# An eighth depth pair by seven products in the late heads, and a third raw weight buffer in the room of the descriptor reserve

## The chip, the cores and the metric

The kernel runs on one core of a Trainium2 chip. The metric is the device time in microseconds of one execution, as the median of several runs. TensorE (PE in the profile, its weight loads PEld), VectorE (DVE), ScalarE (ACT), GpSimd (POOL) and the queue of SyncE (SP), which issues all transfers, each work through their own list of instructions in a fixed order.

## The reference

Two layers over 512 tokens of width 2048, each a sandwich-normalised mixer with an adaptive shift, scale and gate from a conditioning vector. The first is an mLSTM with eight heads, the second an attention over a band of chunks with sixteen heads, which reads keys and values computed from the residual stream after the first layer. All matrices are float32. The part that the change touches is the first layer's input projection:

```python
proj = h @ w_in
qk = jax.nn.silu(causal_conv(proj[..., :A_V0], conv_w, conv_b))
v = proj[..., A_V0:A_O0]
o = proj[..., A_O0:A_Z0]
z = proj[..., A_Z0:A_G0]
...
y = jax.nn.sigmoid(o) * ht * jax.nn.silu(z)      # ht: the normalised mLSTM output
return y @ w_out
```

`h` is 512 x 2048. Per head there are 256 columns of q, 256 of k, and 512 each of v, o and z.

## The kernel before, in words

**Three matmuls for one.** A float32 product is made of float32r parts: `split` (L202) casts a tile to `hi` on ScalarE and takes the rest as `lo` on VectorE; `mm3` (L276) adds hi x hi, hi x lo and lo x hi.

**The weight stream.** All weights lie in one array in the order in which they are used (`stream`, L73). A piece is 128 x 1024 (some smaller). `raw_load` (L214) issues its transfer from SP into a buffer with the tag `raw`; `wpiece` (L224) makes `hi` and `lo` of it (three buffers each). There are `RAW_BUFS` = 2 raw buffers in the pool `wp`. Where a pool of the current stage is entered as `spare[0]`, every third piece goes to one more raw buffer in that pool: so in the start, the heads up to the q/k columns of head 3, the first output projection, the key stage and the second output projection from its second column group on. From the values of head 3 to the end of head 7, in the attention and in the first group of the second output projection `spare[0]` is `None`, and there are two.

**Seven products for eight.** For a pair of output column blocks (128 columns each) and a pair of depth blocks (k, k+1), with the tokens in two halves, the four block products times two token halves can be had from seven half-length products, as in Winograd's form of Strassen's method. `proj_s` (L319) does it: with `f` of the eight depth pairs by seven products of 256 columns, and the others (`eight`, L338) by four plain products of 512 columns. Each of these products is three matmuls. The four accumulators D, C, A, B are put together after the last piece (L368 on ScalarE, L369 to L377 on VectorE). `pair_pieces` (L50) orders the pieces: with f = 7 the first piece holds one depth pair for seven products and the plain one, the other three hold two pairs for seven products. For each piece the sums of weight blocks are taken on VectorE (L244, L245, L246) into a tile `ws`, whose split (`wsh`, `wsl`) follows that of the piece itself. The sums of input blocks (`h1s`) are made once, by `head_sums` (L708), one depth pair at a call; it also overwrites the second token half of `h1[2k]` with the sum of both blocks.

**V after the sums.** Since that half is overwritten, V (`proj_b`, L295) uses for the tokens of the second half the difference of two weight blocks in place of the second block, for the depth pairs that are already summed (`summed`): L251 makes the difference on VectorE, and its split follows.

**The heads.** Heads 0 to 2 have plain projections. Head 3 (`HALF`) has plain q, k and v; its four o/z column pairs are a ramp with f = 4, 5, 6, 7 (`RAMP`), and a call of `head_sums` at the second piece of a pair raises the number for the next one. Heads 4 to 7, the late heads, have `f = HEAD_PAIRS` = 7 in the two q/k pairs and in the four o/z pairs. A head's order on TensorE is q/k, V with the scores, o/z, the denominators and the mixing `ps_n`, then the next head's q/k with the sum of squares (`ps_q`) put in between. After it VectorE takes a reciprocal (L872) and scales the head's output (L874), and SP stores it (L875). Later stages are the output projection, values, keys (f = 6, 7, then 8), attention (f = 8 for all 16 heads) and the second output projection.

**Who sets the order.** A planner in the compiler orders each engine's instructions once, from a cost model, priorities and the free buffers; `tc.high_priority(AHEAD)` moves weight work and the accumulators' reading forward, `pin` and `keep_in_program_order` fix an order. On the chip the lists are followed as they stand.

**Memory.** The program's constructor is called without a size for the dynamic DMA scratch, which reserves 16 KB of each partition for descriptors.

Of the kernel before, what the change touches and what calls it, by code (L numbers as in the profile page):

```python
# [9 lines left out]
F32 = mybir.dt.float32  # L10
# [5 lines left out]
P = 128  # L16
# [14 lines left out]
REL = 257  # L31
EXTW = 640
AHEAD = 300
RAW_BUFS = 2

PAIRS = [(0, 1), (2, 3)]
BLOCKS = [(0, 2), (2, 6), (6, 12), (12, 16)]
# [3 lines left out]


KEY_PAIRS = [6, 7, 8, 8, 8, 8, 8, 8]
HEAD_PAIRS = 7
RAMP = [4, 5, 6, 7]
HALF = 3
ATT_PAIRS = 8
# [25 lines left out]
def stream():  # L73
# [25 lines left out]
    for h in range(NH):  # L99
        for c in (h * DK, V0 // 2 + h * DK):  # L100
# [3 lines left out]
            elif h > HALF:  # L104
                tile_s("a_w_in", c, c + P, HEAD_PAIRS, True)
        tile_b("a_w_in", V0 + h * DV)
        if h >= HALF:
            for i in range(4):
                tile_s("a_w_in", O0 + h * DV + i * P, Z0 + h * DV + i * P, HEAD_PAIRS if h > HALF else RAMP[i], True)
        elif h:  # L110
# [36 lines left out]
def hybrid_trunk(ctx, tc, xT, xN, c, adaT, cols, wst, wg, ext, kc, out):  # L147
    nc = tc.nc
# [8 lines left out]
    def pool(name, bufs=1, **kw):  # L157
        return tc.tile_pool(name=name, bufs=bufs, reuse_waits="tile", **kw)

    wp = ctx.enter_context(tc.tile_pool(name="wp", bufs=3, side="right"))  # L160
# [46 lines left out]

    parted, first, stock = [None, None], [], []
    ahead = [0]
    spare = [None]  # L210
    loads = []
    pin = tc.keep_in_program_order

    def raw_load(keep=lambda ins: ins):  # L214

        i, at = wpos
        n = sum(w for _, _, w in order[i][1])
        wpos[:] = i + 1, at + P * n
        own = spare[0] and i % (RAW_BUFS + 1) == 0
        raw = (spare[0] if own else wp).tile([P, 1024], F32, tag="raw", name=f"wr{i}", bufs=1 if own else RAW_BUFS)[:, :n]  # L220
        keep(nc.sync.dma_start(raw, wst[at : at + P * n].rearrange("(p n) -> p n", p=P)))
        loads.append(raw)

    def wpiece(mat, groups=(), pl=None, bufs=(2, 2), diff=False, early=False):  # L224

        if stock and not early:
            return stock.pop(0)()
        i = wpos[0] - len(loads)  # L230
        m, blocks = order[i]
        assert m == mat
        n = sum(w for _, _, w in blocks)
        with tc.high_priority(ahead[0]):
            if not loads:
                raw_load()
            raw = loads.pop(0)
            ts = []
            c0 = 0
            for j, ns in enumerate(groups):  # L240
                w = ns * P
                r = raw[:, c0 : c0 + 4 * w]
                t = pl.tile([P, 3 * w], F32, tag="ws", name=f"ws{i}_{j}", bufs=bufs[0])
                nc.vector.tensor_tensor(t[:, : 2 * w], r[:, w : 3 * w], r[:, : 2 * w], op=ALU.subtract)  # L244
                nc.vector.tensor_tensor(r[:, w : 2 * w], t[:, w : 2 * w], r[:, :w], op=ALU.add)  # L245
                nc.vector.tensor_tensor(t[:, 2 * w :], r[:, 3 * w :], r[:, w : 2 * w], op=ALU.subtract)  # L246
                ts.append(t)
                c0 += 4 * w
            if diff:
                t = pl.tile([P, n // 2], F32, tag="ws", name=f"ws{i}", bufs=1)  # L250
                nc.vector.tensor_tensor(t, raw[:, n // 2 :], raw[:, : n // 2], op=ALU.subtract)  # L251
                ts.append(t)
            hi = wp.tile([P, 1024], F32R, tag="hi", name=f"wh{i}")[:, :n]
            lo = wp.tile([P, 1024], F32R, tag="lo", name=f"wl{i}")[:, :n]
            if i == 0:
                pin(nc.scalar.copy(hi, raw))

                def rest():
                    parted[0] = nc.vector.tensor_tensor(lo, raw, hi.bitcast(F32), op=ALU.subtract)
                    behind(parted[0], first[0])  # L260
                    return [(hi, lo)]

                return rest
            parted[:] = split(hi, lo, raw, *first[1:] if i < 3 else ())
            out = [(hi, lo)]
            for j, t in enumerate(ts):
                sh = pl.tile(list(t.shape), F32R, tag="wsh", name=f"wsh{i}_{j}", bufs=bufs[1])
                sl = pl.tile(list(t.shape), F32R, tag="wsl", name=f"wsl{i}_{j}", bufs=bufs[1])
                split(sh, sl, t)
                out.append((sh, sl))  # L270
        return out
# [151 lines left out]
    mst = ExitStack()  # L423
# [4 lines left out]
    hst = ExitStack()  # L428
    acp = hst.enter_context(pool("acc"))
    st = ExitStack()  # L430
    sp = spare[0] = st.enter_context(pool("start"))
    def ada_load(i, p, n, pin=lambda ins: ins, parts=1, js=None):

        w = D // parts
# [34 lines left out]
    for q in range(4):  # L469
        t = sp.tile([P, 4, S], F32, name=f"xt{q}")  # L470
# [68 lines left out]
    h1 = []  # L539
# [25 lines left out]
    for n, step in enumerate(steps):  # L565
# [22 lines left out]
        k0, k1, i0, g = step  # L588
# [11 lines left out]
    st.close()  # L600
    ahead[0] = AHEAD

    bp = spare[0] = mst.enter_context(pool("ada1", side="right"))
    hp = hst.enter_context(pool("head"))
    aT = hp.tile([P, 4, NH], F32, name="aT")
    ones_r = hp.tile([P, P], F32R, name="ones_r")
# [99 lines left out]
    h1s = []  # L706

    def head_sums():  # L708
# [3 lines left out]
        for t in h1[2 * k : 2 * k + 2]:  # L712
            r = tp.tile([P, S], F32, tag="t", name=f"h1r{k}_{len(raw)}")
            nc.vector.tensor_tensor(r, t[:, 0, :].bitcast(F32), t[:, 1, :].bitcast(F32), op=ALU.add)
            raw.append(r)
        h1s.append(three_sums(raw, hq, f"h1s{k}", HEAD_PAIRS, h1[2 * k][:, :, 256:]))

    def pair(c, name, other, f=HEAD_PAIRS, at={}):
        z1, z2 = (acp.tile([P, 2, 256], F32, tag="so", name=f"{name}_{i}", bufs=6) for i in range(2))
        proj_s("a_w_in", h1, h1s, f, z1, z2, name, hq, (1, 2), at, True, other)  # L720
        return [z.rearrange("p a t -> p (a t)") for z in (z1, z2)]

    def scores(h, j, qk, pr, nm, nmd, tot):
# [30 lines left out]
    for h in range(NH):  # L754
# [18 lines left out]
        if h == HALF:  # L773
            while loaded or pending:
                background(2)
            spare[0] = None
            mst.close()
            hqst = ExitStack()
            hq = hqst.enter_context(pool("hq", side="right"))
# [13 lines left out]
        at = {8 + 2 * j: lambda j=j: scores(h, j, qk, pr, nm, nmd, tot) for j in range(4)} if h else {}  # L793
# [13 lines left out]
        for m in range(4):  # L807
            with tc.high_priority(AHEAD):
                if m < 3:
                    t = hp.tile([P, 2, S], F32R, tag="qk", name=f"v{h}_{m}", bufs=4)  # L810
                    split(t[:, 0, :], t[:, 1, :], pv[m])
                else:
                    t = hp.tile([P, S], F32, tag="nm", name=f"v{h}_{m}")
# [6 lines left out]
        for i in range(4):  # L820
            if h >= HALF:
                f = HEAD_PAIRS if h > HALF else RAMP[i]
# [65 lines left out]
    tst = ExitStack()  # L888
    tp = tst.enter_context(pool("t2", bufs=6, side="right"))
    rst = ExitStack()  # L890
    rp = spare[0] = rst.enter_context(pool("rp", bufs=12, side="right"))

    ys = []

    def y_tile(k):
        while len(ys) <= k:
            h, q = divmod(len(ys) // 2, 2)
            with tc.high_priority(AHEAD):
                if len(ys) < 4:
                    raw = wp.tile([P, 2, S], F32, tag="raw", name=f"yr{h}_{q}", bufs=RAW_BUFS)  # L900
                    nc.sync.dma_start(raw, ysc[h, :, 2 * q : 2 * q + 2, :])
# [127 lines left out]
    for pair, ms in enumerate(PAIRS):  # L1029
        for g in range(1, 4):  # L1030
            at = scale_steps(4, 12, 20, *([28] if g < 3 else [])) if pair == 0 else {}
            if pair == 0 and g == 3:
                at[28] = lambda: (scale_sums(), amul_cols(2, 48 + KT, GPRE + KT))
            if pair == 1 and g == 1:
                at = {2: lambda: residual(0), 4: lambda: residual(1)}
                at |= {20 + 4 * i: lambda i=i: turned(0, [i], False) for i in range(3)}
            if pair == 1 and g == 2:
                at = {2: lambda: turned(0, [3], False)}
            if pair == 1 and g == 3:
                at = {k: lambda k=k: [key_input(i, kept(i, slice(0, 2 * P)), slice(0, 2 * P)) for i in range(k // 2 - 1, k // 2 + 1)] for k in range(2, 32, 4)}  # L1040
# [48 lines left out]
    for pair, ms in enumerate(PAIRS):  # L1089
        for g in range(2):  # L1090
# [1 line left out]
            if pair:  # L1092
                turn = {k: input_sums for k in (2, 6, 12)}
            values(g, ms, turn)
    spare[0] = None
    rst.close()
    zst = ExitStack()
    zp = zst.enter_context(pool("zp", bufs=2, side="right"))
    zxst = ExitStack()
    zx = zxst.enter_context(pool("zx", side="right"))  # L1100
    for i in range(KT // 2):
        z = zp.tile([P, 4, 256], F32, tag="z", name=f"zk{i}")
        ready = len(hs)
        at = {2: input_sums} if ready < KT // 2 else {}
        assert ready == KEY_PAIRS[i]
        spare[0] = zp
        proj_s("kv_w", hkv, hs, ready, z[:, 0:2, :], z[:, 2:4, :], f"k{i}", zx, (2, 2), at, True, i % 2 == 1)
        nc.sync.dma_start(ksc[i].rearrange("p a t -> p (a t)"), z.rearrange("p a t -> p (a t)"))
    zxst.close()
# [3 lines left out]
    for g in range(2, 4):  # L1113
        n = -(-ATT_PAIRS // 2)
# [3 lines left out]
    for k in range(0, KT, 2):  # L1118
        raw = []
# [9 lines left out]
            h2s[k // 2][0] = h2[k][:, :, 256:]  # L1129
        for i in range(2):  # L1130
            split(h2[k + i][:, 0, :], h2[k + i][:, 1, :], raw[i])
    spare[0] = None
    zst.close()
    tst.close()

# [1 line left out]
    at = ast.enter_context(pool("att"))  # L1137
# [122 lines left out]
    rp = ost.enter_context(pool("x2", bufs=8))  # L1260
# [11 lines left out]
    def y2_tile(k):  # L1272
        while len(y2) <= k:
            i = len(y2) // 2
            raw = wp.tile([P, 2, S], F32, tag="raw", name=f"y2r{i}", bufs=RAW_BUFS) if i < 2 else op.tile([P, 2, S], F32, tag="yr", name=f"y2r{i}", bufs=2)
            with tc.high_priority(AHEAD):
# [45 lines left out]
        3: {0: lambda: gate_part(0), 2: lambda: (gate_row(1, 3), fetch_x(3)), 6: lambda: gate_row(1, 0, late[1]), 12: gate_first},  # L1322
    }
    for g in range(4):
        if g:
            spare[0] = rp
        for pair in [range(4)] if g < 3 else PAIRS:
            ps = [newp(f"ps_y1_{g}_{m}") for m in pair]
            at = {4: lambda: finish(0), 6: lambda: finish(1)} if pair == PAIRS[1] else {}
            add_at(at, gate_steps[g] if pair != PAIRS[1] else {})  # L1330
            proj_b("b_w_out", y2_tile, ps, ms=pair, at=at, late=3 if pair == PAIRS[1] else 0)
            with tc.high_priority(AHEAD):
                for p, m in zip(ps, pair):
                    yo[m].append(op.tile([P, S], F32, tag="o", name=f"yo{m}_{g}"))
                    evac(p, m, g, yo[m][g], g > 0, last if g == 3 and pair == PAIRS[1] else None)
# [59 lines left out]
```

## Time and profile before

| | |
|---|---|
| median of 3 runs | 2782.41 us |
| lowest and highest | 2779.46 and 2782.7 us |
| the profiled execution, span from the first to the last instruction | 2780.8 us |
| TensorE busy | 2757.6 us (99%), 16186 matmuls |
| VectorE busy | 2180.5 us (78%) |
| ScalarE busy | 1388.8 us (50%) |
| HBM | 190 GB/s over the span |

What the profiled execution took around its span is not shown on the page. Busy time of TensorE is modelled from pipelined matmuls, so the time that one matmul costs in a stream is read from the number of matmuls in a stretch without holes, not from the mean duration of one. In rows of busy time by stage the columns are: the stretch in microseconds from the span's start, its length, then for TensorE, weight loads, VectorE, ScalarE and GpSimd the busy time and (x) the number of instructions, the granted clock of TensorE, the DMA engines' busy share and GB/s. In rows of the order of work they are: start, duration, engine, line, operation, output and inputs, shapes, and in brackets the engine's idle time before it and what ended it.

### The profile page before, as it was taken

The numbers are of one execution on the slowest core, as the hardware profiler recorded it, in microseconds if no ns is written. First come the engines' busy times: TensorE is split into PE (matmuls) and PEld (weight loads), VectorE is DVE, ScalarE is ACT, GpSimd is POOL, SyncE is SP. The second block draws the span as 40 slices with busy tenths as digits, with TensorE's granted clock in tenths as the row PEclk, the third lists the DMA queues.
The fourth block names the chain that finished last, engine by engine and source line by source line (L and its number), as shares of the span: only waits on it lengthen the run. The fifth ranks groups of instructions, "written<-read, shape, count | busy, mean of one in ns | idle before, by whom it ended". The sixth has DMA issues, their size and how long they took to land.

```text
span 2780.8 us, 41974 instructions
## 1 busy us (share of the span) xinstructions
PE 2757.6 (99%) x16186; PEld 2446.3 (88%) x16186; DVE 2180.5 (78%) x3421; ACT 1388.8 (50%) x1993; POOL 0.2 (0%) x4
## 2 busy tenths in 40 slices
PE   8999999999999999999999999999999999999998
PEld 6887888888998989989999888888998899999877
DVE  8975978669897887878878676567976788898666
ACT  4243624234554554555645334568534466666523
POOL 0000000000000000000000000000000000000000
PEclk9999999999999999999999999999999999999999
DMA  9754687855233232232326799788535534334686
GB/s 367 292 202 136 246 303 265 300 205 195 92 116 106 100 123 98 101 116 102 120 93 215 236 293 301 250 269 286 175 130 187 162 129 129 125 124 129 214 308 243
DMA packets 167874, 527.05 MB, mean 190 GB/s; under 512 B 17989, under 2 KB 33893, under 8 KB 155001
## 3 DMA queue, kind: packets, MB, share of 16 engines
q1 hardware_dynamic: 167674, 524.38, 54.6%
q8 instruction: 126, 2.06, 0.3%
q14 instruction: 74, 0.61, 0.1%
HBM read 490.69 MB, written 38.85 MB: 190 GB/s over the span
## 4 chain that ended last, share of the span: by engine, by line
PE 91%; DVE 5%; DMA 3%; issue 1%; ACT 1%; SPq 0%; DVEq 0%; ACTq 0%
PE ps_y L274 17%; PE ps_v L274 12%; PE ps_kv L274 5%; PE ps_azo L274 5%; PE ps_o L274 4%; PE ps_czo L274 3%; PE ps_dzo L274 3%; PE ps_az L274 3%; PE ps_cz L274 3%; PE ps_dz L274 3%; PE ps_qk L274 3%; PE ps_z L274 3%; PE ps_l L274 3%; PE ps_bzo L274 3%; PE ps_s L274 2%; PE ps_n L274 2%
## 5 line engine op out<-in xcount | busy, mean ns | idle before, releaser
L203 ACT CAST wh<-wr 128x1024 fp32r<-128x1024 f32 (+1 forms) x560 | 580.0, 1037 | 734.9 <-PE ps_y L274 217.0
L203 DVE TENSOR_TENSOR wl<-wr,wh 128x1024 fp32r<-128x1024 f32 (+1 forms) x560 | 674.5, 1206 | 337.2 <-ACT wh L203 335.6
L274 PE MATMUL ps_y<-wh,y 128*128 128x512 f32 x1536 | 476.7, 390 | 0.5 <-ACT sqy L927 0.5
L274 PEld LDWEIGHTS ps_y<-wh,y 128*128 128x128 f32 x1536 | 288.2, 188 | 60.8 <-ACT sqy L927 1.0
L203 ACT CAST wsh<-ws 128x768 fp32r<-128x768 f32 (+2 forms) x236 | 178.8, 757 | 260.4 <-PE ps_az L274 124.0
L274 PE MATMUL ps_y<-wl,y 128*128 128x512 f32 x768 | 299.0, 389 | 0.0
L274 PE MATMUL ps_v<-wh,h 128*128 128x512 f32 x912 | 289.6, 390 | 0.0
L203 DVE TENSOR_TENSOR wsl<-ws,wsh 128x768 fp32r<-128x768 f32 (+2 forms) x236 | 203.0, 860 | 72.8 <-ACT wsh L203 71.3
L445 DVE CUSTOM_DVE_ANT_0 ada<-ada,scB,cl 128x2048 f32<-128x2048 f32 (+1 forms) x96 | 222.6, 2325 | 18.3 <-DMA ada<-in_adaT 18.3
L274 PEld LDWEIGHTS ps_v<-wh,h 128*128 128x128 f32 x912 | 171.2, 188 | 34.9
L274 PE MATMUL ps_v<-wl,h 128*128 128x512 f32 x456 | 177.9, 390 | 0.0
L274 PEld LDWEIGHTS ps_y<-wl,y 128*128 128x128 f32 x768 | 144.3, 188 | 29.3
L274 PE MATMUL ps_kv<-wh,hkv 128*128 128x512 f32 x512 | 159.3, 390 | 0.0
L244 DVE TENSOR_TENSOR ws<-wr 128x256 f32<-128x256 f32 (+1 forms) x208 | 133.1, 640 | 7.2 <-DMA wr<-in_wst 5.3
L274 PEld LDWEIGHTS ps_kv<-wh,hkv 128*128 128x128 f32 x512 | 96.1, 188 | 19.7
L274 PEld LDWEIGHTS ps_v<-wl,h 128*128 128x128 f32 x456 | 85.7, 188 | 17.8 <-issue 0.9
L274 PE MATMUL ps_kv<-wl,hkv 128*128 128x512 f32 x256 | 99.7, 390 | 0.0
L274 PE MATMUL ps_l<-h,wh 128*128 128x512 f32 x320 | 98.5, 390 | 0.0
L246 DVE TENSOR_TENSOR ws<-wr 128x128 f32<-128x128 f32 (+1 forms) x208 | 83.0, 399 | 4.0
L245 DVE TENSOR_TENSOR wr<-ws,wr 128x128 f32<-128x128 f32 (+1 forms) x208 | 82.6, 397 | 2.9
L274 PE MATMUL ps_azo<-h,wh 128*128 128x256 f32 (+1 forms) x372 | 84.1, 314 | 0.0
L274 PE MATMUL ps_qk<-h,wh 128*128 128x512 f32 x256 | 79.3, 390 | 0.0
(408 smaller groups left out, 6354.1 us busy)
## 6 DMA issues: line engine op xcount, KB each, us to landing
wr<-in_wst SPq DMA_DIRECT2D x530, 512.0 KB, 3.5
ada<-in_adaT SPq DMA_DIRECT2D x94, 1024.0 KB, 6.3
ada<-in_adaT SPq DMA_DIRECT2D x36, 512.0 KB, 7.6
adq<-in_adaT SPq DMA_DIRECT2D x64, 256.0 KB, 4.7
xt<-nsc SPq DMA_DIRECT2D x48, 256.0 KB, 4.3
wr<-in_wst SPq DMA_DIRECT2D x26, 384.0 KB, 3.1
yr<-ysc SPq DMA_DIRECT2D x28, 256.0 KB, 7.1
bsc<-in_ext SPq DMA_DIRECT2D x16, 320.0 KB, 5.1
```

The costliest lines, as they stand in the source:

```text
L203: ins = nc.scalar.copy(hi, src), nc.vector.tensor_tensor(lo, src, hi.bitcast(F32), op=ALU.subtract)
L244: nc.vector.tensor_tensor(t[:, : 2 * w], r[:, w : 3 * w], r[:, : 2 * w], op=ALU.subtract)
L245: nc.vector.tensor_tensor(r[:, w : 2 * w], t[:, w : 2 * w], r[:, :w], op=ALU.add)
L246: nc.vector.tensor_tensor(t[:, 2 * w :], r[:, 3 * w :], r[:, w : 2 * w], op=ALU.subtract)
L274: return nc.tensor.matmul(ps, a, b, start=start, stop=stop)
L445: pin(nc.vector.tensor_tensor_reduce(c, c, (sc or scB)[:, j * w : (j + 1) * w], 1.0, mod[:, i : i + 1] if j else col(CB + i), ALU.mult, AL ...
```

## The change

The reserve for descriptors goes from 16 KB to 1 KB of each partition. `HEAD_PAIRS` goes from 7 to 8: all depth pairs of the late heads' q/k and o/z columns go by seven products, V of these heads takes eight differences instead of seven, and the ramp of head 3 calls `head_sums` once more, in its last pair. The raw buffers are three everywhere, all in `wp`, and the lent buffer (`spare`) goes. The sums' tile `ws` has two buffers in the late heads instead of one.

```diff
-RAW_BUFS = 2
+RAW_BUFS = 3
...
-HEAD_PAIRS = 7
+HEAD_PAIRS = 8
...
-        own = spare[0] and i % (RAW_BUFS + 1) == 0
-        raw = (spare[0] if own else wp).tile([P, 1024], F32, tag="raw", name=f"wr{i}", bufs=1 if own else RAW_BUFS)[:, :n]
+        raw = wp.tile([P, 1024], F32, tag="raw", name=f"wr{i}", bufs=RAW_BUFS)[:, :n]
...
-                t = pl.tile([P, n // 2], F32, tag="ws", name=f"ws{i}", bufs=1)
+                t = pl.tile([P, n // 2], F32, tag="ws", name=f"ws{i}", bufs=2)
...
-        proj_s("a_w_in", h1, h1s, f, z1, z2, name, hq, (1, 2), at, True, other)
+        proj_s("a_w_in", h1, h1s, f, z1, z2, name, hq, (2, 2), at, True, other)
...
-    nc = bacc.Bacc("TRN2", target_bir_lowering=False, num_devices=1)
+    nc = bacc.Bacc("TRN2", target_bir_lowering=False, num_devices=1, dynamic_dma_scratch_size=1024)
```

The other lines of the diff take out the assignments to `spare[0]`.

More of the change, by code (lines that the diff above doesn't have):

```diff
@@ L209, in hybrid_trunk @@
     ahead = [0]
-    spare = [None]
     loads = []
@@ L430, in hybrid_trunk @@
     st = ExitStack()
-    sp = spare[0] = st.enter_context(pool("start"))
+    sp = st.enter_context(pool("start"))
     def ada_load(i, p, n, pin=lambda ins: ins, parts=1, js=None):
@@ L601, in hybrid_trunk @@
     ahead[0] = AHEAD
-    bp = spare[0] = mst.enter_context(pool("ada1", side="right"))
+    bp = mst.enter_context(pool("ada1", side="right"))
     hp = hst.enter_context(pool("head"))
@@ L775, in hybrid_trunk @@
                 background(2)
-            spare[0] = None
             mst.close()
@@ L890, in hybrid_trunk @@
     rst = ExitStack()
-    rp = spare[0] = rst.enter_context(pool("rp", bufs=12, side="right"))
+    rp = rst.enter_context(pool("rp", bufs=12, side="right"))
     ys = []
@@ L1094, in hybrid_trunk @@
             values(g, ms, turn)
-    spare[0] = None
     rst.close()
@@ L1105, in hybrid_trunk @@
         assert ready == KEY_PAIRS[i]
-        spare[0] = zp
         proj_s("kv_w", hkv, hs, ready, z[:, 0:2, :], z[:, 2:4, :], f"k{i}", zx, (2, 2), at, True, i % 2 == 1)
@@ L1131, in hybrid_trunk @@
             split(h2[k + i][:, 0, :], h2[k + i][:, 1, :], raw[i])
-    spare[0] = None
     zst.close()
@@ L1324, in hybrid_trunk @@
     for g in range(4):
-        if g:
-            spare[0] = rp
         for pair in [range(4)] if g < 3 else PAIRS:
```

## The prediction

> **What bounds the kernel now.** I read the page's busy line and clock, then the busy time by stage, then who waits for whom on TensorE, then the order of work where TensorE waits. First the page: busy microseconds, share of the span, instructions; the granted clock in 40 slices.
>
> ```profile
> span 2780.8 us, 41974 instructions
> PE 2757.6 (99%) x16186; PEld 2446.3 (88%) x16186; DVE 2180.5 (78%) x3421; ACT 1388.8 (50%) x1993; POOL 0.2 (0%) x4
> PEclk9999999999999999999999999999999999999999
> ```
>
> TensorE is occupied 99% of the span at full clock. A gain must therefore be matmul time removed, or one of the few holes; 23 us are not busy. The stages (length; PE, weight loads, DVE, ACT busy with instruction counts; clock; DMA share; GB/s) show where:
>
> ```profile
> 0.00:200.00 200.00, 190.92 (x789) 150.20 (x790) 170.85 (x216) 78.36 (x103) 0.20 (x4) 1.00 0.76 294
> 700.00:1502.00 802.00, 800.62 (x5471) 747.49 (x5469) 653.12 (x1041) 432.14 (x564) 0.00 (x0) 1.00 0.32 108
> 2600.00:2781.00 181.00, 170.14 (x757) 139.47 (x755) 116.38 (x164) 56.81 (x89) 0.00 (x0) 0.99 0.74 257
> 1550.00:1700.00 150.00, 150.00 (x664) 124.20 (x663) 101.15 (x171) 55.59 (x64) 0.00 (x0) 1.00 0.84 277
> 2010.00:2090.00 80.00, 80.00 (x669) 80.00 (x668) 65.04 (x105) 29.83 (x36) 0.00 (x0) 1.00 0.37 132
> 2300.00:2500.00 200.00, 200.00 (x1610) 197.69 (x1609) 180.95 (x398) 130.83 (x226) 0.00 (x0) 1.00 0.40 128
> 874.40:956.40 82.00, 82.00 (x640) 79.95 (x639) 63.96 (x103) 40.98 (x49) 0.00 (x0) 1.00 0.29 98
> 956.40:963.50 7.10, 7.10 (x45) 6.57 (x44) 7.05 (x12) 5.93 (x8) 0.00 (x0) 1.00 0.30 97
> 963.50:1006.40 42.90, 42.44 (x324) 40.70 (x323) 39.61 (x62) 22.42 (x30) 0.00 (x0) 1.00 0.31 107
> 1006.40:1053.90 47.50, 47.50 (x219) 39.69 (x218) 35.54 (x56) 27.28 (x40) 0.00 (x0) 1.00 0.36 123
> 694.80:778.10 83.30, 83.30 (x586) 78.31 (x585) 70.43 (x132) 43.38 (x59) 0.00 (x0) 1.00 0.28 97
> 1502.00:1940.00 438.00, 437.49 (x1962) 362.33 (x1962) 294.12 (x439) 237.66 (x356) 0.00 (x0) 1.00 0.83 276
> ```
>
> Row 2 is the late heads, from the ramp of head 3 to the end of head 7: almost no hole. Row 4 has 512-column matmuls only, row 5 is the key stage where all eight depth pairs go by seven products (256 columns only), row 6 the attention stage, likewise eight. Rows 7 to 10 are one head: its four o/z column pairs, the mixing of head 4, the q/k pairs and V of head 5. Row 11 is the ramp, row 12 the first projection with the values.
>
> **Part 1: the eighth pair by seven products.** Each of the 24 column pairs of heads 4 to 7 (two q/k and four o/z pairs per head) drops 12 matmuls of 512 columns and gains 21 of 256. The rate comes from rows 4 and 5: 150.00/664 = 225.9 ns and 80.00/669 = 119.6 ns. Per column pair 12 x 0.2259 = 2.711 us goes and 21 x 0.1196 = 2.511 us comes: 0.200 us saved, and 24 x 0.200 = 4.8 us in all. TensorE has nothing else in these stretches, so this lies on the path. A 256-column matmul costs more than half of a 512 one, since in row 5 the weight loads are as busy as the matmuls (80.00 of 80.00); that is why removing an eighth of one pair's arithmetic yields so little.
>
> The Trainium skill, "TensorE: Matmul & The Clock Gate", section "Back-to-back issue gap", gives a warm gap of N/2.4 + 2.5 ns, 109 and 216 ns here; by that estimate the term would be 24 x (12 x 216 - 21 x 109) ns = 7.3 us. The trace's 119.6 and 225.9 ns differ from it, and I use the trace.
>
> **Part 2: what VectorE and ScalarE do for it.** The first weight piece of a column pair held one depth pair by seven products and one plain; now it holds two. Its three sums and their split grow by these rows of the o/z stretch (count, busy, mean ns, idle before):
>
> ```profile
> L244 DVE TENSOR_TENSOR ws<-wr 128x512 f32<-128x512 f32 x4 | 2.8, 689 | 0.1
> L244 DVE TENSOR_TENSOR ws<-wr 128x256 f32<-128x256 f32 x1 | 0.4, 426 | 0.0
> L245 DVE TENSOR_TENSOR wr<-ws,wr 128x256 f32<-128x256 f32 x4 | 1.7, 423 | 0.1
> L245 DVE TENSOR_TENSOR wr<-ws,wr 128x128 f32<-128x128 f32 x1 | 0.3, 292 | 0.0
> L203 DVE TENSOR_TENSOR wsl<-ws,wsh 128x768 fp32r<-128x768 f32 x4 | 3.8, 952 | 0.0
> L203 DVE TENSOR_TENSOR wsl<-ws,wsh 128x384 fp32r<-128x384 f32 x1 | 0.6, 559 | 0.0
> L375 DVE TENSOR_TENSOR zo<-zo,ps_bzo 128x512 f32<-128x512 f32 x2 | 1.4, 682 | 0.0
> L377 DVE TENSOR_TENSOR zk<-zk,ps_bk x6: 418/419/421, 2008.9 to 2109.4; 128x256 f32<-128x256 f32 x6
> ```
>
> L246 has L245's shapes. Extra: 0.263 + 2 x 0.131 + 0.393 = 0.92 us; the last addition at the end shrinks from 0.682 to 0.419 (L377 takes L375's place), so +0.66 us of DVE per column pair, 15.7 us in 24. V of each late head gets one more difference of 512 columns (0.69 us) and its split (taken as 0.69, the same size): 1.4 us per head, 5.5 us. The eighth sums of the inputs, one more call in the ramp's last pair, are two 512 additions, a 512 split and six 256 operations at about 0.42: 4.6 us. DVE gets 26 us in a stretch of 802 with 653 busy. I cost it at nothing: in o/z it goes to 66.6 of 81.2, in V to 36.9 of 47.5, and the ramp (70.43 of 83.30, three such sums in it already, no hole) has 12.9 us free for 4.6. The attention row is the nearest case: all pairs by seven products, DVE 90% busy, PE 200.00 of 200.00. The sums overwrite half of an input that the ramp pair's first piece reads, so DVE has one more wait for TensorE there, with the next piece's split behind it; the ramp has three of these already and no hole. If that cover goes, each microsecond that DVE is behind is one of TensorE.
>
> The cover is thin in one place, mixing plus q/k: 46.66 of 50.0 us before, 46.66 + 2 x 0.66 = 48.0 of 49.6 after. ScalarE is at 28 of 50 there and stays covered.
>
> **Part 3: third raw, second sums buffer.** Where a later pool lent a third raw buffer (start, early heads, first output projection, key stage, most of the last projection) the count stays three: no change. It becomes three instead of two in the late heads, in attention and in the first group of the last projection. Attention has no hole to fill. What the late heads have is in the waits of TensorE (total, times, longest) and the order of work at head 5's second q/k pair:
>
> ```profile
> PEld ps_dzq L274 <- DVE wl L203: 2.6, 6, 0.6
> PEld ps_q L274 <- ACT sp_q L203: 0.9, 5, 0.2
> PEld ps_gg L701 <- DVE ggate L699: 2.8, 2, 2.4
> 977.04 0.90 DVE L203 TENSOR_TENSOR wsl<-ws,wsh 128x768 fp32r<-128x768 f32 x1
> 978.45 0.42 DVE L244 TENSOR_TENSOR ws<-wr 128x256 f32<-128x256 f32 x1
> 979.38 0.28 DVE L245 TENSOR_TENSOR wr<-ws,wr 128x128 f32<-128x128 f32 x1
> 981.32 0.37 ACT L368 COPY zq<-ps_dzq 128x256 f32<-128x256 f32 x1 [6.49 <-PE ps_dzq L274]
> 981.73 0.42 DVE L369 TENSOR_TENSOR zq<-zq,ps_dzq 128x256 f32<-128x256 f32 x1 [1.46 <-ACT zq L368]
> 983.53 1.22 DVE L203 TENSOR_TENSOR wl<-wr,wh 128x1024 fp32r<-128x1024 f32 x1
> 972.03 0.33 SPq L221 DMA_DIRECT2D wr<-in_wst  x1
> 978.55 4.75 SPq L875 DMA_DIRECT2D ysc<-zo  x4
> 984.78 12.57 SPq L221 DMA_DIRECT2D wr<-in_wst  x3
> ```
>
> The chain: the one sums buffer is free only after the split at 977.04, so the next sums begin at 978.45; the cast of that piece then stands behind L368 on ScalarE, and VectorE idles 1.46 us at L369 with the piece's split (983.53) behind it. Weight loads come later still: the next load is issued at 984.78, after the four stores of the old head. The weights' lead is spent, and TensorE waits for wl six times, 2.6 us in all. With a second sums buffer the sums can run when the raw piece has landed, and with a third raw the loads of 972.03 and 984.78 move one piece earlier, ahead of the stores. That offers the 1.46 us idle and 1.53 us of sums per piece (0.69 + 2 x 0.42) done before the squeeze, against 0.66 us more work and 0.4 us less time. I take 1.8 us of the 2.6 as gained. The ends: all 2.6 gained, or nothing gained and 0.66 + 0.4 = 1.1 us more per head, 4.4 us lost in four. I lie near the gain because the chain above is broken at its first link. Loads moved ahead of the stores on SP delay these by one issue of 0.33 us each; they are read only in the output projection. The L699 wait follows columns loaded for the gate, not these buffers: zero, with 2.8 us either way as a bound, since the planner orders that stretch anew.
>
> **Part 4: the reserve of 1 KB.** The transfers go through one hardware queue, and GpSimd does four memsets at the start:
>
> ```profile
> q1 hardware_dynamic: 167674, 524.38, 54.6%
> ```
>
> I cost it at nothing; a loss is a rival below. The Trainium skill, "DMA: Bandwidth & Descriptors", section "Terms", says that the software path writes descriptors to rings in SBUF and the hardware path feeds the engines directly; no run shown here varies the reserve.
>
> **The sum.** -4.8 - 1.8 + 0 = -6.6 us against the profiled 2780.8, so a span near 2774.2. The span lies 1.6 us under the median of the runs, 2782.41, and inside their spread. I predict 2782.4 - 6.6 = 2775.8 us. About 0.2% (5.6 us) is what a measurement can tell from no change, and the forecast lies barely beyond it.
>
> **Rivals.**
> *The products pay and the buffers do not.* The extra 0.66 us and earlier matmuls keep the waits as they are, or they move to another place. For it: the lead is bounded by three hi/lo buffers too, which stay. Against it: the idle 1.46 us. It gives 2782.4 - 4.8 = 2777.6, down to no gain if the 4.4 us bound holds (2782.0). Chance 0.33: no measurable change.
>
> *Weight sums ahead of the head's end: slower.* Weight work has the planner's priority, the sum of squares behind ps_q has not. With free buffers two pieces' sums (2 x 1.53 = 3.06 us) can be put ahead of it on VectorE, which is full there (7.05 of 7.10); TensorE then waits at ps_q in four heads: 12.2 us, net +7.4, 2789.8 us. It outweighs the saving from 1.2 us per head on. For it: TensorE already waits there by 0.9 us in all. Against it: the planner can put ps_q behind another piece. Chance 0.13.
>
> *Weight loads not hidden.* Nine more loads per column pair at 0.192 us would cost 24 x 9 x 0.192 = 41.5 us, less 768 columns at 225.9/512 ns each, 8.1 us: 2816 us.
>
> ```profile
> L274 PEld LDWEIGHTS ps_dzq<-h1s,wh x112: 186/192/193, 785.2 to 1361.1; 128*128 128x128 f32 x112
> ```
>
> Against it: 669 loads of 0.192 us do not fit in 80.00 us one after another, and row 5 has them. Chance 0.01. The Trainium skill, TensorE page as above, section "The mechanism", says that loads overlap matmuls in flight only where the row group differs, or into the background weight buffer; read without its second half it would be this rival, and the trace disagrees.
>
> *The reserve throttles the queue.* If landings grew from the page's 3.5 us for a 512 KB piece, rows 1 and 12 (DMA share 0.76 and 0.83) would go first; 1% of 200 + 438 us there is 6.4 us, about 2784.0 net. Only hardware_dynamic speaks against it. Chance 0.02; it goes with slower or no change.
>
> ```profile
> wr<-in_wst SPq DMA_DIRECT2D x530, 512.0 KB, 3.5
> ```
>
> **How the numbers follow.** Forecast 0.51, products only 0.33, slower 0.13, the last two 0.03. The forecast's own range is -5.6 to -9 us. Faster 0.50, same 0.36, slower 0.14. The range 2770 to 2783 reaches from the forecast with the 2.8 us of L699 gained too (and some 3 us of spread between runs) to the products-only case with its bound; it leaves out the slower case and little else.
>
> **What would show it.** TensorE instructions 16186 + 24 x 9 = 16402. Row 7's stretch shorter by 0.8 us. DVE busy near 2206. Waits of ps_dzq for wl under 1 us; the idle before L369 in heads 5 to 7 gone; wr loads issued ahead of the ysc stores. Wrong if ps_q waits over 1 us per head, if attention shows holes, or if landings of wr rise clearly above 3.5 us.

## The result, and the profile after

The changed kernel takes 2772.58 us in the median (2771.84 to 2775.16, 7 runs), the kernel before 2782.26 us beside it (2779.46 to 2782.7, 7 runs). The ratio is 0.997, with a 95% interval of 0.996 to 0.9981: faster by 0.3%. The medians differ by 9.7 us, the ratio stands for 8.3 us of 2780, and 6.6 had been forecast. The page of the changed kernel, busy time and the weight landings (line numbers are two or three lower than before):

```profile
span 2770.1 us, 42407 instructions
PE 2749.6 (99%) x16402; PEld 2451.6 (89%) x16402; DVE 2199.7 (79%) x3438; ACT 1399.4 (51%) x2000; POOL 0.2 (0%) x4
wr<-in_wst SPq DMA_DIRECT2D x530, 512.0 KB, 3.7
```

The span is 10.7 us shorter in these two executions. TensorE has the 216 more instructions that were forecast, and is busy for 8 us less. Busy time by stage, columns as before:

```profile
700.00:1490.00 790.00, 790.00 (x5668) 750.30 (x5667) 669.72 (x1054) 443.31 (x572) 0.00 (x0) 1.00 0.34 111
1550.00:1700.00 150.00, 150.00 (x663) 124.20 (x663) 96.72 (x153) 56.63 (x65) 0.00 (x0) 1.00 0.84 272
2010.00:2090.00 80.00, 80.00 (x669) 80.00 (x669) 64.07 (x101) 29.45 (x36) 0.00 (x0) 1.00 0.39 130
2300.00:2500.00 200.00, 200.00 (x1616) 197.87 (x1615) 181.00 (x397) 130.42 (x229) 0.00 (x0) 1.00 0.43 127
```

Busy time shows no hole in the late heads now (790.00 of 790.00); the other stages run at the rates of before. A good yardstick for the late heads is the time from the first mixing matmul `ps_n` of head 3 to that of head 7, four head lengths. In the order of work on TensorE, before:

```profile
778.07 0.62 PE L274 MATMUL ps_n<-p,v 128*128 128x512 f32 x2
1494.79 0.39 PE L274 MATMUL ps_n<-p,v 128*128 128x512 f32 x1
```

and after:

```profile
777.90 0.39 PE L272 MATMUL ps_n<-p,v 128*128 128x512 f32 x1
1485.25 0.62 PE L272 MATMUL ps_n<-p,v 128*128 128x512 f32 x2
```

Four heads take 716.72 us before and 707.35 after: 9.37 of the 10.7 us lie here. The products account for 4.8 by the prediction's sum. Measured, they account for a little more: the o/z columns of one head, four column pairs without a wait in the view, take 81.98 us before (874.39 to 956.37) and 81.10 after (873.76 to 954.86). That is 0.22 us per pair and 5.3 in 24. What is left of the 9.37, 4.1 to 4.6 us, is waits. In these four heads the waits view of TensorE has, before (`ps_dzq` is the accumulator D of a q/k pair, `ps_q` the sum of squares)

```profile
PEld ps_dzq L274 <- DVE wl L203: 2.6, 6, 0.6
PEld ps_q L274 <- ACT sp_q L203: 0.6, 4, 0.2
```

and after the change none. The place where the chain was shown before, head 5's second q/k pair, on VectorE, then ScalarE, then SP:

```profile
975.43 0.89 DVE L203 TENSOR_TENSOR wsl<-ws,wsh 128x768 fp32r<-128x768 f32 x1
976.24 1.21 DVE L203 TENSOR_TENSOR wl<-wr,wh 128x1024 fp32r<-128x1024 f32 x1
979.01 0.68 DVE L242 TENSOR_TENSOR ws<-wr 128x512 f32<-128x512 f32 x1
979.91 0.42 DVE L367 TENSOR_TENSOR zq<-zq,ps_dzq 128x256 f32<-128x256 f32 x1 [0.22 <-ACT zq L366]
979.51 0.37 ACT L366 COPY zq<-ps_dzq 128x256 f32<-128x256 f32 x1 [1.40 <-PE ps_dzq L272]
970.54 13.55 SPq L219 DMA_DIRECT2D wr<-in_wst  x3
986.50 1.26 SPq L872 DMA_DIRECT2D ysc<-zo  x2
```

The idle of 1.46 us ahead of the first addition is 0.22; a split `wl` that had stood behind that addition now stands ahead of it, at 976.24; the stores begin at 986.50, behind three weight loads. The chain that the prediction shows ends at the split of 983.53, and TensorE does not wait for that one. It waits at 991.19 and 997.05 for the next two, which VectorE begins at 989.91 and 995.77, behind the additions and steps of the convolution `cv`:

```profile
995.77 1.22 DVE L203 TENSOR_TENSOR wl<-wr,wh 128x1024 fp32r<-128x1024 f32 x1
```

### The profile page after: what moved, and what is told of

It is laid out like the page before. It is cut to its first block, busy times and chain, and to the rows that moved or that the text cites. A ratio compares the mean times of both kernels' runs of the same rounds, so it can differ in the third digit from the quotient of the medians.

```text
span 2770.1 us, 42407 instructions
## 1 busy us (share of the span) xinstructions
PE 2749.6 (99%) x16402; PEld 2451.6 (89%) x16402; DVE 2199.7 (79%) x3438; ACT 1399.4 (51%) x2000; POOL 0.2 (0%) x4
## 4 chain that ended last, share of the span: by engine, by line
PE 93%; DVE 3%; DMA 2%; issue 1%; ACT 1%; SPq 0%; DVEq 0%; ACTq 0%
PE ps_y L272 18%; PE ps_v L272 12%; PE ps_kv L272 4%; PE ps_azo L272 4%; PE ps_o L272 4%; PE ps_czo L272 4%; PE ps_dzo L272 4%; PE ps_az L272 3%; PE ps_cz L272 3%; PE ps_dz L272 3%; PE ps_qk L272 3%; PE ps_z L272 3%; PE ps_l L272 3%; PE ps_bzo L272 2%; PE ps_s L272 2%; PE ps_n L272 2%
## 5 line engine op out<-in xcount | busy, mean ns | idle before, releaser
L203 ACT CAST wsh<-ws 128x768 fp32r<-128x768 f32 (+2 forms) x240 | 189.1, 788 | 394.6 <-issue 170.3
L203 DVE TENSOR_TENSOR wsl<-ws,wsh 128x768 fp32r<-128x768 f32 (+2 forms) x240 | 215.3, 897 | 104.5 <-ACT wsh L203 102.5
L242 DVE TENSOR_TENSOR ws<-wr 128x512 f32<-128x512 f32 (+1 forms) x208 | 138.9, 668 | 4.1 <-DMA wr<-in_wst 3.9
L244 DVE TENSOR_TENSOR ws<-wr 128x256 f32<-128x256 f32 (+1 forms) x208 | 85.8, 413 | 3.4
L243 DVE TENSOR_TENSOR wr<-ws,wr 128x256 f32<-128x256 f32 (+1 forms) x208 | 85.4, 411 | 2.6
L272 PE MATMUL ps_o<-h,wh 128*128 128x512 f32 x256 | 79.2, 389 | 0.0
```

The source lines that it names most:

```text
L203: ins = nc.scalar.copy(hi, src), nc.vector.tensor_tensor(lo, src, hi.bitcast(F32), op=ALU.subtract)
L272: return nc.tensor.matmul(ps, a, b, start=start, stop=stop)
```

## The experiments

The theory from the prediction: the products pay 4.8 us, and the waits of the second q/k pair end because the second sums buffer and the third raw buffer let weight work go ahead. Rivals: the buffers do nothing, or only one of them does, or the planner's order changed for another reason.

### The products without the buffers

The kernel before with

```diff
-HEAD_PAIRS = 7
+HEAD_PAIRS = 8
...
+ dynamic_dma_scratch_size=1024
```

> The kernel before with the 1 KB reserve and eight pairs by seven products, but two raw buffers with the lent one, and one sums buffer. Theory (the products pay 4.8 us, and the buffers are what takes the waits of the second q/k pair away): 2777 to 2782 us, that is 0 to 5 us under the kernel before; TensorE waits for wl at ps_dzq stay at 2.6 us or grow towards 7. Rival (the waits went because the planner's order changed with the pieces of two groups, whatever the buffers): 2772 to 2774 us, waits for wl at ps_dzq under 0.5 us.

Measured: 2780.8 us against 2780.57 of the kernel before, ratio 1.0001 (0.9992 to 1.001). Waits of TensorE, and the ends of the four heads:

```profile
PEld ps_dzq L274 <- DVE wl L203: 4.6, 8, 0.6
PEld ps_dzq L274 <- ACT wh L203: 2.3, 4, 0.6
777.98 0.39 PE L274 MATMUL ps_n<-p,v 128*128 128x512 f32 x1
1494.20 0.62 PE L274 MATMUL ps_n<-p,v 128*128 128x512 f32 x2
```

The waits grow from 2.6 to 6.9 us, now in all four heads, and the four heads take 716.22 us: 0.50 less than before where 4.8 of matmul time is gone. The products alone bring nothing. The prediction had this as a bound (0.66 us more DVE work and 0.4 us less time per head, 4.4 us in four), and 4.3 us are lost (4.8 by the measured 0.22 us per pair).

### The buffers without the products

The changed kernel with

```diff
-HEAD_PAIRS = 8
+HEAD_PAIRS = 7
```

> The changed kernel with seven depth pairs by seven products in the late heads, as before; three raw and two sums buffers. Theory: the products' 4.8 us are missing and the waits are gone: 2776 to 2778.5 us, waits of ps_dzq for wl under 0.5 us. Rival (buffers do nothing by themselves): 2781 to 2783 us, waits near 2.6 us.

Measured: 2776.76 us, ratio 0.9987 (0.9978 to 0.9996). No wait of `ps_dzq` for `wl` is left, but a small new one has come, `ps_q` for the sum of squares:

```profile
PEld ps_q L272 <- DVE sp_q L203: 1.3, 5, 0.3
```

Four of these five waits lie in the late heads, 1.1 us in all, where the kernel before has 0.6. Behind head 4 the split of a weight piece's sums (966.44 on VectorE) now stands ahead of the split of the sum of squares (967.32). That is like the mechanism of the slower rival, at less than a tenth of the 12.2 us put on it.

### One sums buffer, three raw; two sums buffers, two raw

In the changed kernel, the first:

```diff
-                t = pl.tile([P, n // 2], F32, tag="ws", name=f"ws{i}", bufs=2)
+                t = pl.tile([P, n // 2], F32, tag="ws", name=f"ws{i}", bufs=1)
...
-        proj_s("a_w_in", h1, h1s, f, z1, z2, name, hq, (2, 2), at, True, other)
+        proj_s("a_w_in", h1, h1s, f, z1, z2, name, hq, (1, 2), at, True, other)
```

> The changed kernel with one sums buffer in the late heads, three raw. Theory (the second sums buffer is the first link): the waits of ps_dzq for wl come back, 2.6 us or more, and the time is 2775 to 2778 us. Rival (the third raw buffer is the lever, through earlier loads): 2772 to 2773.5 us, waits under 0.5 us.

The second is `products_only` with the same two lines at 2, and with the lent raw buffer as before the change.

> The kernel before with the 1 KB reserve, eight pairs and two sums buffers, but two raw buffers with the lent one. Theory (the sums buffer is the first link): most of the waits of ps_dzq for wl are gone, under 1 us, 2772 to 2775 us. Rival (the third raw buffer is the lever): waits of 2.6 us or more, 2776 to 2780 us.

Measured: one sums buffer 2783.74 us, ratio 1.0012 (1.0004 to 1.0021), a little slower than the kernel before and above what either expectation had (2772 to 2778); two raw buffers 2773.23 us, ratio 0.9975 (0.9966 to 0.9983), like the whole change. With one sums buffer the waits are the ones of `products_only`, although there are three raw buffers, and the old picture is back (VectorE, then ScalarE, head 5):

```profile
977.54 0.94 DVE L203 TENSOR_TENSOR wsl<-ws,wsh 128x768 fp32r<-128x768 f32 x1
979.00 0.68 DVE L242 TENSOR_TENSOR ws<-wr 128x512 f32<-128x512 f32 x1
982.00 0.42 DVE L367 TENSOR_TENSOR zq<-zq,ps_dzq 128x256 f32<-128x256 f32 x1 [1.37 <-ACT zq L366]
983.93 1.22 DVE L203 TENSOR_TENSOR wl<-wr,wh 128x1024 fp32r<-128x1024 f32 x1
981.59 0.37 ACT L366 COPY zq<-ps_dzq 128x256 f32<-128x256 f32 x1 [6.49 <-PE ps_dzq L272]
```

With two raw buffers and two sums buffers the four heads end as in the changed kernel, at 1485.31 instead of 1485.25:

```profile
778.02 0.39 PE L274 MATMUL ps_n<-p,v 128*128 128x512 f32 x1
1485.31 0.39 PE L274 MATMUL ps_n<-p,v 128*128 128x512 f32 x1
```

The third raw buffer has no part in the gain of the late heads.

Outside them it is not free with one sums buffer. `one_ws` has the same four heads as `products_only` (716.24 and 716.22 us) and takes 2.9 us more in all (2783.74 against 2780.80). Its profile shows part of that: a wait of 2.4 us in the mixing at the end of head 7, for `dd`, a denominator that ScalarE makes. The kernel before and `products_only` have no wait for `dd` there:

```profile
PEld ps_n L272 <- ACT dd L847: 2.6, 2, 2.4
```

Why `dd` is late there was not looked into.

### Two sums buffers alone

The kernel before with the reserve of 1 KB and the two lines of the sums buffer at 2.

> The kernel before with the 1 KB reserve and two sums buffers in the late heads, seven pairs by seven products, two raw buffers with the lent one. Theory (the single sums buffer is the first link of the late heads' waits, at seven pairs as well): the waits of ps_dzq for wl under 0.5 us, 4 us less time in the late heads, 2776 to 2778 us. Rival (it needs the third raw buffer too when the first piece has one group): the waits stay above 1.5 us, 2779 to 2782 us.

Measured: 2777.74 us, ratio 0.9989 (0.998 to 0.9998). The waits of `ps_dzq` are gone, `ps_q` waits 1.3 us as in the kernel with both buffers and seven pairs. This run leaves one place of the design empty. Microseconds from the first `ps_n` of head 3 to that of head 7, as read from the orders of work:

| | 7 pairs | 8 pairs |
|---|---|---|
| one sums buffer, two raw | 716.72 (before) | 716.22 |
| one sums buffer, three raw | not run | 716.24 |
| two sums buffers, two raw | 712.80 | 707.29 |
| two sums buffers, three raw | 712.77 | 707.35 (after) |

The second sums buffer is worth 3.9 us with seven pairs and 8.9 with eight. The products are worth 0.5 us with one sums buffer and 5.5 with two (5.3 by the measured 0.22 us per pair). The raw buffer is worth nothing in these heads.

### The reserve alone

> The kernel before with the reserve of 1 KB alone. Theory (the transfers do not use that room): no change, ratio 0.999 to 1.001, landings of wr at 3.5 us, the same order of work. Rival (the smaller reserve throttles the queue or moves buffers to worse places): 0.1% or more slower, landings of wr longer.

The kernel before with the constructor's line of the change and nothing else. Measured: 2780.28 us, ratio 0.9997 (0.9988 to 1.0006), landings of the 512 KB pieces 3.6 us in the median. The order of the instructions on TensorE, VectorE and ScalarE is the same, and a few early loads on SP have other places. The reserve costs nothing that can be measured.

### Is it the buffer, or the order of the work?

A buffer can let an instruction start sooner on the chip, or let the planner put VectorE's and ScalarE's work in another order. To see whether the order alone does it, with one sums buffer, the reading of the q/k pairs' accumulators was put off:

```diff
-        with tc.high_priority(AHEAD):
+        with tc.high_priority(0 if name.startswith("zq") else AHEAD):
             nc.scalar.copy(z1[:, 0, :], D[:, h0])
             ... the additions on VectorE ...
```

> The kernel with three raw buffers, one sums buffer and eight pairs, as in one_ws, but the reading of the q/k pairs' accumulators (the copy on ScalarE and the additions on VectorE) without the planner's priority. Theory (second link: the next pair's cast stands behind the copy L366 on ScalarE, and VectorE idles at L367): the weight work goes ahead, the waits of ps_dzq for wl and wh fall from 6.9 us to under 3, and the time from 2783.7 to 2776 to 2779 us. Rival (with one sums buffer the weight work has no room to go ahead, whatever the priority; or the convolutions now come too late for the scores): the waits stay above 5 us, 2781 us or more.

> The kernel of products_only (1 KB reserve, eight pairs, two raw buffers with the lent one, one sums buffer) with the q/k pairs' accumulators read without the planner's priority. Theory (the order of VectorE's work decides, and neither buffer is needed for it): the waits of ps_dzq for wl and wh under 1 us instead of 6.9, 2772 to 2776 us instead of 2780.8. Rival (it took the third raw buffer to let the weight work go ahead): waits above 3 us, 2778 to 2781 us.

Measured: with three raw and one sums buffer 2773.83 us, ratio 0.9974 (0.9963 to 0.9984); with neither buffer 2771.44 us, ratio 0.9967 (0.9955 to 0.9979). That is the whole gain, without the second sums buffer and without the third raw. No wait of `ps_dzq` is left, and the four heads take 706.94 us. VectorE, ScalarE and TensorE of the kernel with neither buffer:

```profile
980.52 1.22 DVE L203 TENSOR_TENSOR wl<-wr,wh 128x1024 fp32r<-128x1024 f32 x1 [0.76 <-ACT wh L203]
981.66 0.95 DVE L203 TENSOR_TENSOR wsl<-ws,wsh 128x768 fp32r<-128x768 f32 x1
982.53 0.41 DVE L369 TENSOR_TENSOR zq<-zq,ps_dzq 128x256 f32<-128x256 f32 x1
979.17 0.37 ACT L368 COPY zq<-ps_dzq 128x256 f32<-128x256 f32 x1 [6.49 <-PE ps_dzq L274]
984.24 1.05 ACT L203 CAST wh<-wr 128x1024 fp32r<-128x1024 f32 x1 [3.02 <-DVE wr L245]
988.24 1.52 ACT L658 ACTIVATE cv<-zq,cl 128x512 f32<-128x512 f32 x2 [2.21 <-DVE zq L373]
777.88 0.39 PE L274 MATMUL ps_n<-p,v 128*128 128x512 f32 x1
1484.82 0.62 PE L274 MATMUL ps_n<-p,v 128*128 128x512 f32 x2
```

ScalarE still idles 6.49 us with the next cast behind its copy, and TensorE waits for nothing, so that idle cost nothing. What differs is the order behind it. On VectorE the weights' splits at 980.52 and 981.66 come ahead of the addition at 982.53 and its followers, instead of behind them. On ScalarE the cast of the piece after that (984.24) now comes ahead of the convolution (988.24). In `products_only`, the same kernel without the lower priority, it comes behind:

```profile
986.36 1.53 ACT L658 ACTIVATE cv<-zq,cl 128x512 f32<-128x512 f32 x2 [2.82 <-DVE zq L373]
989.37 1.05 ACT L203 CAST wh<-wr 128x1024 fp32r<-128x1024 f32 x1 [1.48 <-DVE wr L245]
```

Before, VectorE waited for the copy in front of work that TensorE needed sooner. The priority moved work on both engines, and no run tells the one from the other. The third raw buffer again costs something outside the four heads: these take 706.96 us with it and 706.94 without, and the whole 2773.83 against 2771.44.

### Two more holes

Left in the changed kernel are waits in the stretch before the keys (`ps_kv`) and for the gate columns in the last projection (`ps_gg`). In the last projection the four turns of the gate columns (`gate_part`) were moved one step of two depth blocks later:

```diff
-... 6: lambda: gate_part(1), ...   2: {2: lambda: (gate_part(2), gate_sums()), ... 8: lambda: gate_part(3), 10: gate_sums, ...   3: {0: lambda: gate_part(0), ...
+... 8: lambda: gate_part(1), ...   2: {2: gate_sums, 4: lambda: (gate_part(2), fetch_x(1)), ... 10: lambda: (gate_part(3), gate_sums()), ...   3: {2: lambda: (gate_part(0), ...
```

> The changed kernel with the three turns of the gate columns in the last projection one step of two depth blocks later. Theory (TensorE waits there for the gate's column sums, which are just late): the waits of ps_gg, 2.6 us, fall under 0.5 us, and the time is 2770 to 2771.5 us. Rival (the sums come later by the same step, or the gate row comes too late for the reading of the accumulators): 2772 to 2775 us.

Measured: 2770.03 us (2769.5 to 2772.37), ratio 0.996 (0.9947 to 0.9974). No wait of `ps_gg` is left. Before the keys, eight instead of six row buffers (`bufs=8` in the pool `t2`) and rows fetched three ahead (`len(fetched) < 3`):

> The changed kernel with eight instead of six row buffers from the output projection to the keys, and the rows for the keys' input sums fetched three ahead instead of two. Theory (ScalarE waits there for the rows' transfers, and the weights' casts stand behind it): the waits of ps_kv and ps_dk for wl, 2.9 us, fall under 1 us, 2770 to 2771.5 us. Rival (VectorE and ScalarE have too much to do in this stretch, whenever the rows land): the waits stay above 2 us, 2772 to 2774 us.

Measured: 2772.31 us, ratio 0.9968 (0.9956 to 0.9981); `ps_kv` waits 2.4 us for `wl` where it waited 2.6. No gain: the rows' landing is not what is late there, or not alone. Both together, and the changed kernel once more beside it:

> The changed kernel with both: the gate's three turns one step later in the last projection, and eight row buffers with rows fetched three ahead before the keys. Theory (the two holes are independent, and each pays by what its waits lose): 2769 to 2770.5 us, waits of ps_gg under 0.5 us and of ps_kv under 2.5 us. Rival (fetching ahead does nothing for the keys, as its own timed runs say): 2770 us, as with the later gate alone.

> The changed kernel once more, unaltered, beside the combined one on the same chip. Theory (the holes before the keys and in the last projection depend on when transfers land, and differ from one execution to the next of the same instructions): 2772 to 2773 us, the waits in the late heads as in its first profile, those of ps_kv and ps_gg each different by up to 2 us. Rival (they are set by the order of the instructions): the same waits within 0.3 us.

Measured: both together 2770.84 us (2769.76 to 2771.71), ratio 0.9963 (0.995 to 0.9977); the changed kernel 2771.95 us (2770.94 to 2772.24), ratio 0.9966 (0.9954 to 0.9979). The intervals do not part them; the ranges of their runs overlap, with the medians 1.1 us apart. `ps_kv` waits 3.5 us in the combined kernel, where under 2.5 was expected. In the changed kernel's second profile the waits of `ps_kv` and `ps_gg` add up to those of the first within about 0.3 us each, as the rival of that run has it. Waits of the changed kernel, first and second profile:

```profile
PEld ps_kv L272 <- DVE wl L203: 2.6, 3, 1.2
PEld ps_gg L699 <- DVE ggate L697: 1.6, 1, 1.6
PEld ps_gg L699 <- PE ps_y L272: 1.0, 1, 1.0
```

```profile
PEld ps_kv L272 <- DVE wl L203: 2.3, 4, 0.8
PEld ps_gg L699 <- issue: 1.6, 1, 1.6
PEld ps_gg L699 <- DVE ggate L697: 0.5, 1, 0.5
PEld ps_gg L699 <- ACT sqy L924: 0.2, 1, 0.2
```

Other profiles speak against the rival. Up to 2200 us the kernel with the later gate turns has the instructions of the changed kernel in the same order on TensorE, VectorE, ScalarE and SP, yet `ps_kv` waits 1.6 us more than in the first profile above. `reserve_only` has the order of the kernel before on TensorE, VectorE and ScalarE, and waits 2.0 us less for the gate than the 2.8 before. The two rows:

```profile
PEld ps_kv L272 <- DVE wl L203: 4.2, 4, 2.6
PEld ps_gg L701 <- ACT sqy L927: 0.8, 1, 0.8
```

So the order does not fix these holes; they can differ by some 2 us without a change of it.

## Why the prediction was right or wrong

**The direction and the range were right**, 2775.8 against 2772.58 us. The gain of 9.7 us in the medians lies beyond the forecast's own 5.6 to 9, the 8.3 of the ratio near its end.

**Part 1, the products: right.** The rates held (669 matmuls of 256 columns in 80.00 us again). The o/z stretch gives 0.22 us per pair where 0.20 was worked out, since the few 512-column matmuls cost about 229 ns from start to start there and not 225.9. Between the kernels with two sums buffers, seven pairs take 2777.74 and 2776.76 us and eight take 2773.23 and 2772.58: 4.5 and 4.2 us, or 4.4 and 5.9 when each is set against the kernel before beside it, and 4.8 were worked out.

**Part 2, the cover: right about where it is thin, wrong about its cost.** VectorE got 19 us more busy time against 26 worked out from durations. Part of the difference is that busy time counts overlapping instructions once: added up, the durations grow by 23 us. It was costed at nothing. With one sums buffer it costs nearly all that the products bring, as `products_only` shows: 4.3 us, close to the lower end of 4.4 that part 3 had worked out. That they are so close is partly luck: the bound takes the extra work of one q/k pair (0.66 us) with the time saved in two (0.4 us). With the work of both pairs, which part 2 counts, it is 1.7 us per head and 6.9 in four.

**Part 3, the buffers: the mechanism half right, the size wrong.** This is the step that failed. I took 1.8 us; in the changed kernel 4.1 to 4.6 us of waits are gone in the late heads. Three errors lie in it. First, the waits view showed 2.6 us, and I took that as the most that could be gained. It counts the idle time ahead of a weight load alone. In head 5 before (TensorE, and the weight load of the wait):

```profile
995.39 0.50 PE L274 MATMUL ps_dzq<-h1s,wh 128*128 128x256 f32 x2
995.73 0.40 PE L274 MATMUL ps_azq<-h,wh 128*128 128x256 f32 x2
995.97 0.40 PE L274 MATMUL ps_bzq<-h1s,wh 128*128 128x256 f32 x2
996.21 0.47 PE L274 MATMUL ps_czq<-h1s,wsh 128*128 128x256 f32 x2
997.05 0.39 PE L274 MATMUL ps_dzq<-h1s,wl 128*128 128x256 f32 x1 [0.37 <-DVE wl L203]
997.27 0.41 PE L274 MATMUL ps_dzq<-h1s,wh 128*128 128x256 f32 x2
997.05 0.19 PEld L274 LDWEIGHTS ps_dzq<-h1s,wl 128*128 128x128 f32 x1 [0.57 <-DVE wl L203]
```

Two matmuls take 0.24 us from start to start (995.73 to 995.97). From 996.21 it is 0.84, so 0.60 is lost where the matmul's bracket says 0.37 and the weight load's, which the view counts, 0.57. The matmul after the wait takes another 0.22 instead of 0.12, and the first pair at 995.39 took 0.34; the view has neither. Heads 5 to 7 were each 1.47 us longer than 4.8/4 explains (179.47 against 176.80 us), 4.4 us in three, or 4.1 with the measured 0.22 us per pair. The waits view has 2.6 us of `ps_dzq` for them, and 0.5 of `ps_q` that went as well: 3.1 us.

Second, the third raw buffer was credited, and it does nothing: the loads do move ahead of the stores, as forecast, and no one waits for them. In the kernel with neither buffer the four stores again go ahead of the next weight loads (976.71 and 981.77), and TensorE waits for neither. Third, the idle of 6.49 us ahead of the copy L368 on ScalarE, with the next cast behind it, is not a link that costs: it is there in the kernel with neither buffer, which has no wait. What counts is that the weights' splits and casts come ahead of the additions and convolution steps that they stood behind.

**Part 4, the reserve: right**, 0.9997 (0.9988 to 1.0006). The landings of 3.7 us after the change, and 3.5 before, cost nothing that the late heads show.

**The rivals.** "The products pay and the buffers do not" is the reverse of what happened: without the second sums buffer, or the lower priority in its place, the products do not pay. "Weight sums ahead of the head's end" was seen at small size with seven pairs (1.1 us in the late heads against 12.2 priced), and with eight pairs not at all. That weight loads are not hidden is excluded again by 669 loads in 80.00 us.

**Open.** The last projection took part in the differences of single profiles: its waits for the gate turn were 2.8 us before and 2.6 after. I settled neither what sets the holes before the keys nor whether the later gate turns are worth the 1 to 2 us that the medians suggest. One raw buffer more with seven pairs and one sums buffer was not run, nor the lower priority with seven pairs. Which engine's order counts, VectorE's or ScalarE's, was not told apart, and what the third raw buffer costs at the end of head 7 was not followed up.

## What to carry to other kernels

When an engine is covered only just, two edits can each be worth nothing or little alone and much together: here the saved matmuls paid only once the order of the weight work in one tight stretch of 40 us was mended. Before buying a buffer, read the waiting engine's order and ask which instruction stands in front of the late one. Here, with the same products, one priority gave the gain of both buffers and left their room free. And size a wait on TensorE by the distance from start to start, or by the length of the repeated unit, since pipelined durations hide part of it.

## What the runs showed of the hardware that was not expected

After a wait TensorE does not resume at its rate: the matmul after it took 0.22 us to the next start instead of 0.12 (997.05 to 997.27 above, and likewise behind the waits at 991.19, 1176.52 and 1355.98 of the same profile). The waits of three heads, with their restarts, cost 4.1 to 4.4 us where the waits view adds up to 3.1.
